# The second block's mixer: attention blocks, projections and delta steps written out side by side

## Chip, cores and metric

The kernel runs on one core of a Trainium2 chip. The metric is the device time of one execution in microseconds; the median of several runs counts. An engine is named as in the profile: PE (matmuls; PEld its weight loads), DVE (vector), ACT (activation functions), POOL (general vector work), SP (issues most DMAs).

## What is computed

Two transformer blocks of two layers each, over 512 tokens of width 1024, all in float32. The change touches only the mixer of the second block, which runs once in each of its two layers:

```python
u = rms_norm_2(x, pre_mix_w[l]) @ w_in[l]
(u_conv, dq, dk, dv, gqkv, gz, b_f, b_b, a_f, a_b) = jnp.split(u, offs, axis=-1)
y_conv  = conv_module(u_conv, ...)        # 31-tap depthwise convolution, layer norm, silu
y_diff  = diff_attention(dq, dk, dv, ...) # 6 heads: softmax(q1 k1 - slope*dist) - lam * softmax(q2 k2 - slope*dist), times v
y_delta = gated_deltanet(gqkv, gz, ...)   # 6 heads, both directions, chunks of 64: triangular solve, then a scan over 8 chunks
y = concatenate([y_conv, y_diff, y_delta]) @ w_out[l]
x = x + rms_norm_2(y, post_mix_w[l])      # then a feed-forward part of 4096 hidden columns
```

## The kernel before

The method `second(l)` is one layer of the second block. Activations lie feature by feature (128 partitions, 8 groups) as two tiles `hh` and `hl`, the high and low part of each float32; a matmul by a weight is three matmuls (`mm3`, L485 to L487; `bank`, L509, where the order of accumulation is fixed). A **dense unit** (`dense_fm`) is 128 output columns: its weights are loaded into `raw` (two buffers, pool `p_raw`), split into `wh` and `wl` (four buffers each, pool `p_whl`) by ACT, DVE and POOL, and multiplied in 24 matmuls of 512 columns. `dense_tok` makes 384 columns for all tokens in 96 matmuls.

The mixer's own parts, each for pairs of heads f = 0, 1, 2:

- `delta_proj` (three dense units: q, k, v), a 3-tap convolution and Silu, and transposes into `tokq`, `tokk`, `tokv`.
- `delta_prep`: norms, the decay matrices (tiles `E`), the products `KK`, a round through DRAM and the solve of 16x16 triangles (`delta_solve`, L1518 and L1520, 30 small DVE instructions), and the rest (`delta_prep2`: `Aq`, `kd`, `qg`).
- `delta_uw`: the inverse is put together from 16 to 32 to 64 rows, one direction d after the other and in the last stage one chunk c after the other; then U and W.
- `delta_scan`: both directions' chunk states step by step (copies L1650 on DVE, L1652 on ACT), then the output `OI`. `delta_out`: norm, gate, and a transpose into `cat` in DRAM.
- `conv_proj` (four units) and `conv_taps`: 31 taps, half on DVE (L1743), half by ACT (L1746) with POOL (L1747).
- `diff_proj` (six units, parked in DRAM as `qk`) and `diff`: 24 **blocks** (6 heads x 4 query blocks). `scores(b)` is two matmuls (L1840), a bias and minimum on DVE (L1842), Exp on ACT (L1844); `outputs(b)` combines the two halves (L1862 on DVE, or every third by ACT and POOL, L1859 and L1860), transposes (L1866), evacuates to `dat` and multiplies by `dv`.

Only dependences between tiles and the ring of buffers behind each tag are fixed. The order of each engine's instructions is set when the program is built, by a planner that at every moment prefers, of what it holds to be ready, what stands first in the program; so the written order is a priority. Before, `second` writes first all delta and dense work, then the attention. The attention's score tiles `dP` are taken from `p_raw`, its `dqk` and `dat` from `p_whl`, the buffers of the dense weights; its other tiles lie in the pool `rb`, which is opened when `hh` and `hl` are closed and takes their place. PSUM has four rings of two banks: `mm`, `fx`, `ax`, `sA`.

Of the kernel before, what the change touches and what calls it, by code (L numbers as in the profile page):

```python
# [17 lines left out]
P = 128  # L18
# [7 lines left out]
def shape_constants():  # L26
# [74 lines left out]
    c["dist"] = -np.abs(np.arange(896)[None, :] - 384 - i[:, None])  # L101
# [17 lines left out]
BAL = ((0, 0, 0), (0, 0, 0), (0, 0, 0))  # L119
# [56 lines left out]
class Kern:  # L176
# [1152 lines left out]
    def gates(self, l, pool, ps):  # L1329
# [10 lines left out]
        beta, a, e, u, g = T("beta"), T("ga"), T("ge_"), T("gu"), T("gg")  # L1340
# [41 lines left out]
    def delta_proj(self, l, f, pool, hsrc, pss=None):  # L1382

        nc = self.nc
        tok = [pool.tile([P, 4, 2, 64], F32, tag="tok" + n, name="tok" + n, bufs=1 if n == "q" else 2) for n in "qkv"]
# [17 lines left out]
        for z in range(3):  # L1403
# [4 lines left out]
        return tok  # L1408

    def delta_prep(self, l, f, pool, tok, G):  # L1410
# [15 lines left out]
        def normed(z, t):  # L1426
            x = pool.tile([P, 4, P], F32, tag="kq"[z] + "T", name="kq"[z] + "T", bufs=2 - z)
# [38 lines left out]
        KK = [pool.tile([P, 2, 4, 64], F32, tag=f"KK{d}", name="KK", bufs=2) for d in range(2)]  # L1466
# [25 lines left out]
    def delta_prep2(self, l, f, pool, st, E, normed, products, tq, tk, gb):  # L1492

        Aq = [pool.tile([P, 2, 4, 64], F32, tag=f"Aq{d}", name="Aq", bufs=2) for d in range(2)]
        products(normed(1, tq), [(Aq[d], E["q", d]) for d in range(2)])
        kd, qg = [], []
        for d in range(2):
            for lst, t, n, tag in ((kd, tk, "etl", "kd"), (qg, tq, "egc", "qg")):
                k = pool.tile([P, 4, 2, 64], F32, tag=f"{tag}{d}", name=tag, bufs=2)
                self.tt(k, t, gb(n, d), 512, ALU.mult)  # L1500
                lst.append(k)
# [26 lines left out]
    def delta_uw(self, l, f, pool, st, G):  # L1528
# [3 lines left out]
        st["U"], st["W"] = [], []  # L1532
        xd = st["xd"]
        Zs = [pool.tile([P, 8, 64], F32, tag=f"Z{d}", name="Z") for d in range(2)]
        TZ = [pool.tile([P, 2, 8, 32], F32, tag=f"TZ{d}", name="TZ") for d in range(2)]
        half = lambda i, n: self.half[:, i:i + 2].unsqueeze(1).unsqueeze(3).to_broadcast([P, n, 2, 512 // n // 2])
        for d in range(2):
# [5 lines left out]
        VBs = []  # L1543
        for d in range(2):
            v = pool.tile([P, 4, 2, 2, 64], F32, tag=f"VB{d}", name="VB")
            gb = lambda n: G[n][:, :, 6 * d + 2 * f:6 * d + 2 * f + 2].unsqueeze(3).to_broadcast([P, 4, 2, 64])
            self.tt(v[:, :, :, 0], st["tv"], gb("beta"), 512, ALU.mult)
            self.tt(v[:, :, :, 1], st["tk"], gb("beg"), 512, ALU.mult)
            VBs.append(v)
        for d in range(2):  # L1550
            Z, T, KK, VB = Zs[d], TZ[d][:, 0], st["KK"][d], VBs[d]
            hs = slice(6 * d + 2 * f, 6 * d + 2 * f + 2)

            GI = pool.tile([P, 8, 64], F32, tag=f"GI{d}", name="A16")
            self.mul(GI, KK.rearrange("p a b c -> p (a b) c"), self.dmc[:, 3 + d].unsqueeze(1).to_broadcast([P, 8, 64]), 512)
            blocks = [(slice(32 * q, 32 * q + 32), n) for n in range(8) for q in range(4)]
            pq = self.psx([P, 8, 32])
            for b, n in blocks:
                mm(pq[b, n], GI[b, n, b.start % 64:b.start % 64 + 32], T[b, n], start=True, stop=True)
            A = pool.tile([P, 2, 4, 32], F32, tag="Q", name="AT", bufs=2)  # L1560
            if d == 0:
                nc.vector.tensor_tensor(out=A, in0=pq.rearrange("p (h t) a -> p h t a", h=2),
                                        in1=G["beta"][:, :, hs].rearrange("p t h -> p h t").unsqueeze(3).to_broadcast([P, 2, 4, 32]), op=ALU.mult)
            else:
                nc.vector.tensor_copy(A, pq.rearrange("p (h t) a -> p h t a", h=2))
            A = A.rearrange("p h t a -> p (h t) a")
            pz = self.psx([P, 2, 8, 32])
            for b, n in blocks:
                mm(pz[b, 0, n], TZ[d][b, 1, n], A[b, n], start=True, stop=True)
                mm(pz[b, 1, n], A[b, n], TZ[d][b, 1, n], start=True, stop=True)  # L1570
            nc.vector.tensor_tensor(out=TZ[d], in0=TZ[d], in1=pz, op=ALU.subtract)
            self.load["dve"] += 900
            self.tt(Z.rearrange("p n (b j) -> p n b j", b=2), TZ[d][:, 1].unsqueeze(2).to_broadcast([P, 8, 2, 32]), half(0, 8), 512, ALU.mult)
            Q = pool.tile([P, 2, 4, 32], F32, tag="Q", name="Q", bufs=2)
            for c in range(2):
                s0 = 64 * c + 32 * d
                c0 = 64 * c + 32 * (1 - d)
                s_, c_ = slice(s0, s0 + 32), slice(c0, c0 + 32)
                sf, cf = slice(32 * d, 32 * d + 32), slice(32 * (1 - d), 32 * (1 - d) + 32)
                pq = self.psx([P, 2, 4, 32])  # L1580
                for h in range(2):
                    for tt in range(4):
                        mm(pq[c_, h, tt], KK[s_, h, tt, cf], T[s_, 4 * h + tt], start=True, stop=True)
                if d == 0:
                    nc.vector.tensor_tensor(out=Q[c_], in0=pq[c_], in1=G["beta"][c_, :, hs].rearrange("p t h -> p h t").unsqueeze(3)
# [209 lines left out]
    def diff(self, l, pool, qk, vd, cat, between):  # L1795
# [52 lines left out]
        def outputs(b):  # L1848
# [19 lines left out]
            if qb == 0:  # L1868
                s["po"], s["bank"] = self.psum([P, 4, 64]), self.bank()
# [492 lines left out]
```

## Time and profile before

| | |
|---|---|
| median of 3 runs | 4024.43 us (4018.16 to 4025.21) |
| the profiled execution | 4036.42 us; span from its first to its last instruction 4034.6 us |
| instructions | 67160 |
| DMA | 379.79 MB, mean 94 GB/s |

A row of the profile names a source line, an engine, an operation, and the tiles it writes and reads. "Busy" is the time in which the engine ran the instructions of a group, "idle before" the time in which it had nothing to run just before them, with what ended it. PEclk is the share of its full clock that TensorE was granted.

### The profile page before, as it was taken

Reading aid. Unit: us, or ns where it says so; the run is one execution under the profiler, and the core shown is the slowest. Engines: PE = TensorE matmul, PEld = TensorE weight load, DVE = VectorE, ACT = ScalarE, POOL = GpSimd, SP = SyncE. Lnnn points to the kernel's source line nnn. Section 1 sums busy time; section 2 is a strip of 40 time slices with the busy share of each in tenths; the row PEclk is TensorE's granted clock in tenths of the full one; section 3 lists DMA queues with packets and bytes.
Section 4 is the critical chain, followed back from the end, with each engine's and each line's share of the span. In section 5 each row is a group of like instructions: output and inputs, shape, how many; then the busy total and the mean of one; then the engine's idle time right before and its main releaser. Section 6 shows DMA issues by size and latency. Waiting matters only on the chain. (4 is left out here: it accounts for less than half of the span.)

```text
span 4034.6 us, 67160 instructions
## 1 busy us (share of the span) xinstructions
PE 3704.7 (92%) x27441; PEld 3287.6 (81%) x27441; DVE 2440.8 (60%) x4507; ACT 1571.0 (39%) x2654; POOL 1669.0 (41%) x1168
## 2 busy tenths in 40 slices
PE   8999989989998999997999988878999988878998
PEld 6888767989998788887999876768988776778988
DVE  6454566665666333336776684548767685558665
ACT  4544255323223222223343543444434443344433
POOL 2221225455553223233666454215554363115654
PEclk8999879989999999998999987879999887878999
DMA  6322444112222212121232433132334333132333
GB/s 208 93 77 78 155 130 157 43 53 65 72 73 77 66 58 71 60 84 51 84 115 88 118 99 119 52 113 94 105 105 122 92 101 104 55 123 92 105 97 112
DMA packets 420364, 379.79 MB, mean 94 GB/s; under 512 B 64586, under 2 KB 366169, under 8 KB 419161
## 3 DMA queue, kind: packets, MB, share of 16 engines
q1 hardware_dynamic: 414490, 367.01, 29.4%
q10 hardware_dynamic: 5567, 8.49, 0.6%
q8 instruction: 216, 3.54, 0.4%
q14 instruction: 91, 0.75, 0.1%
HBM read 332.21 MB, written 43.25 MB: 93 GB/s over the span
## 5 line engine op out<-in xcount | busy, mean ns | idle before, releaser
L206 ACT CAST wh<-raw 128x1024 fp32r<-128x1024 f32 (+2 forms) x441 | 444.6, 1014 | 630.9 <-PE mm L486 277.6
L233 POOL TENSOR_TENSOR wl<-raw,wh 128x1024 fp32r<-128x1024 f32 (+2 forms) x196 | 468.1, 2397 | 530.7 <-ACT wh L206 476.5
L233 DVE TENSOR_TENSOR wl<-raw,wh 128x1024 fp32r<-128x1024 f32 (+1 forms) x268 | 378.1, 1415 | 189.1 <-ACT wh L206 176.4
L485 PE MATMUL mm<-Hh,wh 128*128 128x512 f32 (+1 forms) x1256 | 417.5, 335 | 15.3 <-DVE x L1033 12.9
L487 PE MATMUL mm<-Hh,wl 128*128 128x512 f32 (+1 forms) x1256 | 417.0, 333 | 0.5 <-DVE wl L233 0.5
L486 PE MATMUL mm<-Hl,wh 128*128 128x512 f32 (+1 forms) x1256 | 416.3, 332 | 0.0
L485 PEld LDWEIGHTS mm<-Hh,wh 128*128 128x128 f32 x1256 | 238.7, 190 | 42.9 <-DVE x L1033 14.3
L487 PEld LDWEIGHTS mm<-Hh,wl 128*128 128x128 f32 x1256 | 238.8, 190 | 26.1 <-DVE wl L233 0.7
L486 PEld LDWEIGHTS mm<-Hl,wh 128*128 128x128 f32 x1256 | 239.0, 190 | 24.3
L485 PE MATMUL mm<-hh,wh 128*128 128x512 f32 (+1 forms) x640 | 231.9, 366 | 16.4 <-DVE hh L208 6.9
L509 PE MATMUL mm<-hl,wh 128*128 128x256 f32 (+1 forms) x808 | 231.5, 290 | 6.4 <-DVE hl L1960 6.3
L509 PE MATMUL mm<-hh,wl 128*128 128x256 f32 (+1 forms) x808 | 231.6, 290 | 5.5 <-DVE wl L233 4.1
L487 PE MATMUL mm<-hh,wl 128*128 128x512 f32 (+1 forms) x640 | 227.2, 357 | 2.8 <-POOL wl L233 2.8
L486 PE MATMUL mm<-hl,wh 128*128 128x512 f32 (+1 forms) x640 | 229.0, 359 | 0.6 <-DVE hl L698 0.6
L509 PE MATMUL mm<-hh,wh 128*128 128x256 f32 (+1 forms) x808 | 218.4, 288 | 6.5 <-ACT hh L1968 3.2
L206 ACT CAST wh<-s 128x1024 fp32r<-128x1024 f32 (+1 forms) x128 | 106.9, 835 | 267.4 <-PE mm L486 137.6
L509 PE MATMUL mm<-th,wh 128*128 128x256 f32 (+1 forms) x644 | 195.3, 305 | 8.1 <-ACT wh L206 5.5
L509 PE MATMUL mm<-th,wl 128*128 128x256 f32 (+1 forms) x644 | 197.3, 307 | 3.1 <-DVE wl L233 3.1
L1033 DVE SCALAR_TENSOR_TENSOR x<-mm,mod,x 128x512 f32<-128x512 f32 (+1 forms) x224 | 138.2, 630 | 99.9 <-PE mm L487 99.4
L509 PE MATMUL mm<-tl,wh 128*128 128x256 f32 (+1 forms) x644 | 195.3, 303 | 0.6 <-DVE tl L233 0.6
L233 POOL TENSOR_TENSOR Hl<-o,Hh 128x1024 fp32r<-128x1024 f32 (+3 forms) x76 | 140.9, 1856 | 92.6 <-ACT Hh L206 91.1
L509 PEld LDWEIGHTS mm<-hl,wh 128*128 128x128 f32 (+1 forms) x808 | 155.8, 193 | 9.7 <-DVE hl L1960 7.7
(737 smaller groups left out, 10886.8 us busy)
## 6 DMA issues: line engine op xcount, KB each, us to landing
raw<-in_w_ff_dram SPq DMA_DIRECT2D x68, 1024.0 KB
raw<-in_ffn_w_in_dram SPq DMA_DIRECT2D x88, 512.0 KB
raw<-in_mod_w_dram SPq DMA_DIRECT2D x40, 1024.0 KB
raw<-in_odd_w_in_dram SPq DMA_DIRECT2D x24, 1024.0 KB
raw<-in_ffn_w_out_dram SPq DMA_DIRECT2D x19, 1024.0 KB
raw<-in_w_in_dram SPq DMA_DIRECT2D x38, 512.0 KB
dqk<-qk SPq DMA_DIRECT2D x48, 256.0 KB
raw<-in_w_out_dram SPq DMA_DIRECT2D x12, 768.0 KB
```

The source lines that it names most:

```text
L206: nc.scalar.copy(hi, src)
L233: i = (nc.vector if e == "dve" else nc.gpsimd).tensor_tensor(out=out, in0=a, in1=b, op=op)
L485: mm(ps, ah, bh, start=first, stop=False)
L486: mm(ps, ah, bl, start=False, stop=False)
L487: mm(ps, al, bh, start=False, stop=last)
L509: i = self.nc.tensor.matmul(out, lhsT, rhs, start=start, stop=stop, skip_group_check=True)
L1033: self.nc.vector.scalar_tensor_tensor(out=x[:, ct, :n], in0=ps, scalar=gate[:, ct:ct + 1], in1=x[:, ct, :n], op0=ALU.mult, op1=ALU.add)
```

## The change

`second` now writes the attention's 24 blocks as the frame of the mixer. A head section makes the gates, f = 0 of the delta projections, the first q and k of the attention and all of `vd`. Then a table `steps` says which other work stands inside block b, between the scores of block b + 1 and the outputs of block b: one dense unit a block at most places, and one delta step.

- The attention has tiles of its own in the pool `dl`: `dqk` (three buffers), `dP` (two, one block each), `dat` (one). The slope is now the scale of the DVE instruction and divided out of q in `diff_proj` (`qs`), so that the biases on POOL go; all 24 combinations are on DVE. The products go into the transposes' bank (`fx`), and each block is scaled on its own (24 small DVE instructions for 6 larger).
- `KK`, `Aq`, `kd`, `qg` and `kqT` have one buffer where they had two.
- `delta_uw` handles both directions, and both chunks, together: one instruction for two or four.
- `conv_taps` stands after the last dense matmul, in `rb`, with four taps a block in blocks 13 to 20 and two buffers for `cm`. The pool `cv` goes.

```diff
-BAL = ((0, 0, 0), (0, 0, 0), (0, 0, 0))
+SLOPES = [2.0 ** -2, 2.0 ** -4, 2.0 ** -6, 2.0 ** -8, 2.0 ** -1, 2.0 ** -3]
...
-        KK = [pool.tile([P, 2, 4, 64], F32, tag=f"KK{d}", name="KK", bufs=2) for d in range(2)]
+        KK = [pool.tile([P, 2, 4, 64], F32, tag=f"KK{d}", name="KK") for d in range(2)]
...
+        A = pool.tile([P, 2, 8, 32], F32, tag="E", name="AT", bufs=5)
+        nc.vector.tensor_tensor(out=A.rearrange("p d n a -> p (d n) a"), in0=pq.rearrange("p d n a -> p (d n) a"),
+                                in1=bb.rearrange("p d h t -> p (d h t)").unsqueeze(2).to_broadcast([P, 16, 32]), op=ALU.mult)
...
+        for d, s_, c_, cf in places:
+            for h, tt in heads:
+                mm(pq[c_, h, tt], KK[d][s_, h, tt, cf], TZ[d][s_, 0, 4 * h + tt], start=True, stop=True)
+        Q = pool.tile([P, 2, 4, 32], F32, tag="Q", name="Q", bufs=2)
+        nc.vector.tensor_tensor(out=Q, in0=pq, in1=bm.unsqueeze(3).to_broadcast([P, 2, 4, 32]), op=ALU.mult)
...
+        def tap(t):
+            nc.vector.scalar_tensor_tensor(out=acc[:, 0], in0=hp[:, 0, t:t + 512], scalar=w(t, 0), in1=acc[:, 0], op0=ALU.mult, op1=ALU.add)
+            m = pool.tile([P, 512], F32, tag="cm", name="cm", bufs=2)
+            nc.scalar.activation(m, hp[:, 1, t:t + 512], AF.Copy, scale=w(t, 1))
+            nc.gpsimd.tensor_tensor(out=acc[:, 1], in0=acc[:, 1], in1=m, op=ALU.add)
...
-                t = self.p_whl.tile([P, 1024], F32R, tag="wh", name="dqk")
+                t = pool.tile([P, 1024], F32R, tag="dqk", name="dqk", bufs=3)
...
-            if b % 2 == 0:
-                blocks[b // 2] = (self.p_raw.tile([P, 2048], F32, tag="raw", name="dP").rearrange("p (q m c) -> p q m c", q=2, m=2),
-                                  self.p_whl.tile([P, 1024], F32R, tag="wl", name="dat").bitcast(F32).rearrange("p (q k c) -> p q k c", q=2, k=4))
-            pe = blocks[b // 2][0][:, b % 2]
+            pe = blocks[b] = pool.tile([P, 2, 512], F32, tag="dP", name="dP", bufs=2)
...
-            if b % 3 == 0:
-                nc.scalar.activation(pe[:, 1], pe[:, 1], AF.Copy, scale=rs[:, 1:2])
-                nc.gpsimd.tensor_tensor(out=pe[:, 0], in0=pe[:, 0], in1=pe[:, 1], op=ALU.add)
...
+            po = pt[:, 0, :64]
             for kb in range(4):
...
+            o = s["o"]
+            nc.vector.tensor_scalar(out=o[:, qb, h], in0=po, scalar1=rs[:, 0:1], scalar2=None, op0=ALU.mult)
...
             if b + 1 < nb:
                 scores(b + 1)
+            for f in steps.get(b, ()):
+                f()
             outputs(b)
...
+        for g in proj(0, pss[1:]):
+            g()
+        dp(0, 0)()
+        dp(0, 1)()
+        self.dense_tok(w, [(1280, 384)], [hs], park(vd), banks=[self.psum, self.psum, self.psf, self.psf])
         prep(0)
...
+        steps = {0: [p1[1]], 1: [p1[2]], 2: [p1[0], do(uw, 0)], 3: [dp(1, 0)], 4: [dp(1, 1), do(scan, 0), do(prep, 1)], 5: [p2[1]],
+                 6: [p2[2], do(uw, 1)], 7: [p2[0], cp(0)], 8: [dp(2, 0), do(scan, 1), do(prep, 2)], 9: [dp(2, 1)], 10: [cp(1), do(uw, 2)],
+                 11: [lambda: self.dense_tok(w, [(2816, 384)], [hs], park(zd, AF.Silu))], 12: [tail, do(out, 0), do(scan, 2)],
+                 13: [t4], 14: [t4, do(out, 1)], 15: [t4], 16: [t4, do(out, 2)], 17: [t4], 18: [t4], 19: [t4], 20: [t4]}
+        self.diff(l, pool, qk, vd, cat, steps, lambda f: None)
```

`proj(f)` gives the three units of `delta_proj`, `dp(f, z)` is `diff_proj` for q (z = 0) or k (z = 1), `cp(z)` is two units of `conv_proj`, `tail` closes `hh` and `hl`, opens `rb` and starts the convolution.

## Rows read from the trace of the kernel before

**Rows 1.** The page's first part: busy us, share of the span, instructions.
```profile
PE 3704.7 (92%) x27441; PEld 3287.6 (81%) x27441; DVE 2440.8 (60%) x4507; ACT 1571.0 (39%) x2654; POOL 1669.0 (41%) x1168
```
**Rows 2.** Windows: stretch, length, busy of five engines, PEclk, DMA share, GB/s.
```profile
2275.00:2455.00 180.00, 160.77 (x1313) 133.23 (x1312) 132.21 (x247) 86.64 (x130) 98.28 (x67) 0.91 0.40 112
2455.00:2641.00 186.00, 153.94 (x2800) 129.96 (x2798) 111.72 (x333) 73.51 (x175) 43.89 (x38) 0.78 0.22 65
2641.00:2687.50 46.50, 27.52 (x108) 22.87 (x108) 23.37 (x71) 18.02 (x33) 5.17 (x6) 0.50 0.45 153
2275.00:2687.50 412.50, 342.23 (x4219) 286.06 (x4217) 267.29 (x650) 178.17 (x337) 147.35 (x110) 0.81 0.33 95
...
3175.00:3585.40 410.40, 338.62 (x4218) 282.32 (x4217) 265.33 (x650) 177.73 (x336) 147.25 (x108) 0.81 0.33 96
...
2612.60:2633.90 21.30, 17.98 (x419) 17.07 (x418) 10.74 (x48) 7.12 (x18) 2.31 (x2) 0.90 0.14 48
...
2340.00:2400.00 60.00, 47.29 (x451) 43.26 (x450) 58.90 (x91) 28.95 (x43) 37.75 (x24) 0.83 0.33 77
```
**Rows 3.** Lines, first mixer, attention: count, busy us, mean ns, idle before, its ender.
```profile
L1844 ACT ACTIVATE dP<-dP,dmx 128x512 f32<-128x512 f32 x48 | 34.5, 720 | 66.5 <-DVE dmx L1842 64.3 <-DVE hy L645 2.2
...
L1842 DVE CUSTOM_DVE_ANT_0 dP<-fx,abias 128x512 f32<-128x512 f32 x48 | 32.5, 686 | 11.2 <-PE fx L1840 10.1 <-POOL abias L1809 0.6
...
L1862 DVE SCALAR_TENSOR_TENSOR dP<-dP,drs 128x512 f32<-128x512 f32 x16 | 14.2, 885 | 0.4
```
**Rows 4.** The same view: the convolution's taps.
```profile
L1747 POOL TENSOR_TENSOR cacc<-cacc,cm 128x512 f32<-128x512 f32 x30 | 43.4, 1448 | 37.0 <-ACT cm L1746 37.0
...
L1743 DVE SCALAR_TENSOR_TENSOR cacc<-hp,dw,cacc 128x512 f32<-128x512 f32 x30 | 32.8, 1094 | 0.7 <-ACT cacc L1739 0.6
```
**Rows 5.** Timeline, PE: dense matmuls in a row; then one block's transposes and products.
```profile
2441.15 0.40 PE L485 MATMUL mm<-hh,wh 128*128 128x512 f32 x1
2441.38 0.39 PE L486 MATMUL mm<-hl,wh 128*128 128x512 f32 x1
...
2603.85 0.66 PE L1866 MATMUL fx<-ident,dP 128*128 128x128 f32 x4
...
2605.91 1.10 PE L509 MATMUL mm<-dv,dat 128*128 128x64 f32 x8
```
**Rows 6.** Timeline, PE: the first mixer's end and the output projection's first matmuls.
```profile
2670.91 1.97 PE L509 MATMUL mm<-dv,dat 128*128 128x64 f32 x8 [0.68 <-ACT dat L243]
2682.95 1.12 PE L1707 MATMUL mm<-ident,do 128*128 128x128 f32 x4 [10.07 <-POOL do L233]
2687.53 2.50 PE L485 MATMUL mm<-hh,wh 128*128 128x512 f32 x5 [3.46 <-DVE hh L208]
```
**Rows 7.** Timeline, several engines: the delta chain of f=0, then of f=2.
```profile
2280.45 0.63 ACT L1417 ACTIVATE dsq<-tokq 128x512 f32<-128x512 f32 x1
...
2379.67 1.04 POOL L233 TENSOR_TENSOR TZ<-T,half 128x512 f32<-128x512 f32 x1 [0.51 <-DMA T<-xd]
...
2459.34 0.40 ACT L1606 ACTIVATE W<-ax 128x256 f32<-128x256 f32 x1
...
2459.50 0.65 PE L1431 MATMUL ax<-ident,tokk 128*128 128x128 f32 x4 [0.69 <-ACT U L243]
...
2495.70 0.62 ACT L1522 COPY chG<-chX 128x256 f32<-128x256 f32 x1 [2.94 <-DVE chX L1520]
...
2576.05 0.83 PE L1559 MATMUL ax<-TZ,A 32*32 32x32 f32 x64 [0.33 <-DVE o2n L644]
...
2612.14 0.40 ACT L1606 ACTIVATE W<-ax 128x256 f32<-128x256 f32 x1
...
2629.03 0.59 ACT L243 COPY OI<-ax 128x512 f32<-128x512 f32 x1 [2.84 <-PE ax L509]
```
**Rows 8.** Lines, ACT, first mixer: loads of function tables.
```profile
L1395 ACT ACT_TABLE_LOAD x2 | 2.6, 1283 | 0.0
...
L1844 ACT ACT_TABLE_LOAD x2 | 2.6, 1283 | 0.0
```

More of the change, by code (lines that the diff above doesn't have):

```diff
@@ L1402, in ev, with step @@
             return g
-        for z in range(3):
+        def step(z):
+            n = "tok" + "qkv"[z]
+            tok[z] = pool.tile([P, 4, 2, 64], F32, tag=n, name=n, bufs=2 if z else 1)
             if pss:
@@ new lines, in delta_uw @@
+        for d, s_, c_, cf in places:
+            o, i = Z[d][s_, :, cf], pz[s_].rearrange("p h t a -> p (h t) a")
+            if d:
+                nc.scalar.activation(o, i, AF.Copy, scale=-1.0)
+            else:
+                nc.vector.tensor_scalar(out=o, in0=i, scalar1=-1.0, scalar2=None, op0=ALU.mult)
+        self.load["dve"] += 3000
+        st["U"], st["W"] = ([pool.tile([P, 4, 2, 64], F32, tag=f"{n}{d}", name=n) for d in dd] for n in "UW")
+        VB = []
+        for d in dd:
@@ L1597, in delta_uw @@
+            VB.append(v)
+        for d in dd:
             for b in range(2):
@@ L1795, in diff, with ev @@
-    def diff(self, l, pool, qk, vd, cat, between):
+        def ev(j, i, ps):
+            hi, lo = (pool.tile([P, 512], F32, tag="pc", name=n, bufs=3) for n in ("dhi", "dlo"))
+            scale = 1.0 if z else self.qs[:, f:f + 1]
+            nc.scalar.activation(hi.bitcast(F32R), ps, AF.Copy, scale=scale)
+            nc.vector.scalar_tensor_tensor(out=lo.bitcast(F32R), in0=ps, scalar=scale, in1=hi, op0=ALU.mult, op1=ALU.subtract)
+            self.load["act"] += 480
+            self.load["dve"] += 662
+            for g in range(4):
+                nc.sync.dma_start(qk[f][z, g], lo if (g % 2, g // 2)[z] else hi)
@@ L2015, in out @@
         def out(f):
[L2016 to L2018 removed]
+            self.delta_out(l, f, late["rb"], OI[f], zd, cat[:, 5 + f], G)
         uw = lambda f: self.delta_uw(l, f, pool, sd[f], G)
[L2020 to L2028 removed]
@@ L2044, in second, with tail @@
-        out(1)
-        scan(2)
-        self.level(0, 0, 100)
-        out(2)
-        self.level(*BAL[2])
-        self.diff(l, rb, qk, vd, cat, lambda f: self.conv_norm(l, rb, acc, cat) if f == 1 else None)
-        p_rb.close()
-        p_cv.close()
+        dp = lambda f, z: lambda: self.diff_proj(l, f, z, pool, hs, qk)
+        cp = lambda z: lambda: self.conv_proj(l, z, pool, hs, hd)
+        do = lambda g, f: lambda: g(f)
+        def tail():
+            p_hs.close()
+            late["st"] = ExitStack()
+            late["rb"] = late["st"].enter_context(tc.tile_pool(name=f"rb{l}", bufs=1, side="right"))
+            late["acc"], late["taps"] = self.conv_taps(l, late["rb"], hd)
@@ new lines, in taps @@
+        def taps(n):
+            for _ in range(min(n, len(late["taps"]))):
+                late["taps"].pop(0)()
+            if not late["taps"] and late["acc"] is not None:
+                self.conv_norm(l, late["rb"], late["acc"], cat)
+                late["acc"] = None
+        for g in proj(0, pss[1:]):
[3 more added lines that the diff above has]
+        self.dense_tok(w, [(1280, 384)], [hs], park(vd), banks=[self.psum, self.psum, self.psf, self.psf])
+        prep(0)
+        p1, p2 = proj(1), proj(2)
```

245 lines of the change are left out of this document (88 added, 157 removed).

## The prediction

> **What bounds the kernel now.** I read the page's shares first [rows 1]. PE is busy for 92% of the span, which sounds like a kernel that only fewer matmuls could shorten. A share is a mean over stages, so next I cut the mixer out with the windows view [rows 2]. The first mixer is followed from 2275 us, when the shared first units are done, to 2687.5 us, when the output projection begins [rows 6]: 412.5 us; the second takes 410.4 us. Together they are a fifth of the span, and here nothing is full: PE 342 us of busy time at a granted clock of 0.81, DVE 267 us, ACT 178, POOL 147.
>
> The windows within it show two halves that lack what the other has. To 2455 us all dense units and much of the delta work run, PE is busy for 0.89 of the time at a clock of 0.91, and DVE for 0.73. From 2455 to 2641 us there is no dense unit left. Attention, scans and the late delta steps share the engines; PE's clock is 0.78, DVE's share 0.60. In the last 46.5 us the clock is 0.50 and both engines are half idle. The attention cannot begin sooner, whatever the planner wants: its tiles come out of `raw`, `wh` and `wl`, which the dense weights use until the last unit. The lines view says what such a stage waits for [rows 3]: ACT stands idle for 66.5 us before the 48 Exps, 64.3 of it until DVE has made the minimum. These are waits of a chain with nothing to put in between, not of a full engine.
>
> **What the mixer needs at least.** Busy time of PE at a low clock is stretched, so I multiply each stage's by its clock: 160.8 x 0.91 + 153.9 x 0.78 + 27.5 x 0.50 = 280 us at full clock (an estimate). At the busy share that PE reached in the first half, 0.89, that is 314 us. DVE's 267 us are less. So up to 98 us of each mixer is waiting that a better mixture could remove.
>
> **The change, part by part.**
>
> *Head section.* After 2275 us come two units of q and k and the 96 matmuls for `vd`. Dense matmuls follow each other every 0.23 us [rows 5]; for 384 columns I scale by 384/512. That is 48 x 0.233 + 96 x 0.175 = 28 us, on PE's path. The first dqk must go through DRAM, and the gates' small tiles now share the ring `E` with `prep(0)`; both delay only chains, under PE's 28 us and the next units. Without that cover each would cost what the chain is late, which no row shows; I set nothing.
>
> *Blocks 0 to 12, with the dense work.* What is left is 14 units and `zd`: 14 x 24 x 0.233 + 16.8 = 95 us, to which attention and delta add. The later blocks' PE work is 11 x 2.23 = 25 us (two scores at 0.233, four transposes 0.66, eight products 1.10 [rows 5]) and 16 us for one scan and the norms, from the window 2612.6 to 2633.9, where they ran nearly alone (18.0 busy at 0.90 [rows 2]). So this stage holds 280 - 28 - 41 = 211 us, at a share of 0.89 237 us.
>
> *Blocks 13 to 23.* No dense matmul is left, so DVE counts: 11 blocks at 2 x 0.686 + 0.885 and about 0.5 of small instructions [rows 3] are 31 us (24 instructions that scale the products, new, lie in that 0.5); 30 taps at 1.094 us [rows 4] are 33; scan, norms and conv_norm twice the 10.7 us of that window, 21. Together 85 us. At the first half's share, 0.73, they take 116 us, at the second half's, 0.60, 142. I take 116: the taps are independent work that can stand in the gaps, as they do in the first half.
>
> *The end.* Before, 16.6 us lie between the last block's products and the first output matmul [rows 6], as norm, transpose, `cat` and the split follow each other. That stays. But `hh` and `hl` no longer lie over the attention's tiles, and `raw` is free: the 48 matmuls on the convolution's rows, 11.2 us, and their weights can go in front. `x`, 2 MB, must now wait for the attention's pool; at the 153 GB/s of the last stretch [rows 2] that is 14 us beside 28 us of output matmuls, so nothing; uncovered it would be 14.
>
> *Edits inside the steps.* `delta_uw` becomes shorter as a chain: for f = 2 it took 36.5 us, 2576.05 to 2612.54, for two directions in turn [rows 7], and should take about half. POOL loses 8 combinations a mixer and the biases, DVE gains 8 x 0.885 = 7 us and loses about as much in `delta_uw`. POOL and ACT are far from full, so I count nothing. Of SP's queue: the same DMAs move; the weight loads now pass the reads of `dqk`, of which the third buffer lets only half of the next head be fetched ahead, so some of the five changes of head can hold SP and the loads behind it. No row prices that; between nothing and five loads late I take nothing, since `raw` has a second buffer.
>
> **The sum.** By parts: 28 + 237 + 116 + 16.6 - 11.2 = 386 us. This takes the stages one after the other. They are not: with tiles of its own the attention can run ahead of its place while PE is full, so DVE's later work moves forward. Were it all mixed, 314 + 16.6 - 11.2 = 319 us. With two `dP` buffers it can be only so far ahead; I take a point nearer the sum by parts, 361 us. Against 412.5 and 410.4 that gives 51.5 + 49.4 = 101 us. The profiled execution took 4036.4 us, so 3935; the median of the runs shown is 0.997 of it, so 3924 us.
>
> **The rivals.**
>
> *Everything mixes* (319 us a mixer): for it, the first half already reaches 0.89 on PE. Against it, this needs PE and DVE both above 0.83 throughout. 4036 - 185 = 3851, as a median 3840.
>
> *Table loads.* Exp, Silu and Sigmoid now alternate. Before, 48 Exps had two loads, of 1.28 us each [rows 8], because the dense evacuations were over. After, six evacuations of `delta_proj`, two of `conv_proj`, one group for `zd` and conv_norm each fall between Exps: 10 visits, 20 loads, 25.7 us a mixer. If all lie on the chain that paces the blocks, 361 becomes 387: 49 us saved, 3975 as a median. For it: ACT waits on the chain already [rows 3]; against it: ACT is busy for 178 of 412 us [rows 2], and a load can go ahead of the data.
> [...]
>
> *No gain.* The dense work runs ahead by itself, as the planner prefers whatever is ready, and the blocks from 13 on are paced as the second half was: 28 + 237 + 142 + 5.4 = 412 us, the time of before; 4024. For it: the planner has the same freedom before and after, and PSUM's `fx` ring of two banks serves scores, transposes, products and delta_proj alike. Against it: the later blocks hold one scan instead of three.
>
> *Slower: the delta chain.* With single `KK`, `kd`, `qg` and `Aq`, step f + 1 cannot pass step f: `prep` waits for `uw`, its rest for `scan`. One turn of f = 2 took 36 us from its first transposes to the solve's end, 36.5 us of `uw`, now half, and 16.5 us of `scan` [rows 7]: 71 us, some 80 with two trips through DRAM. With some 17 us for the last output that is 2280 + 3 x 80 + 17 = 2537, long before the attention's end. But f = 0, which met the taps on a DVE that was busy for 58.9 of 60 us [rows 2], took 179 us to the end of `uw` [rows 7]; with `uw` halved and a scan, 156. Three such turns end at 2765 us, 77 after 2687.5: 155 us slower, 4179 as a median. It decides from 130 us a turn. I expect about 100, as the taps have moved behind.
>
> **How the numbers follow.** Main case, 341 to 386 us a mixer, 0.46 (as medians 3884 to 3974); everything mixes 0.16; table loads 0.12; no gain, 395 to 425 us, 0.15; the chain 0.11. About 0.2% of the time, 8 us, is what a measurement of this kernel can tell from no change. Of "no gain" I give 0.06 to faster, 0.05 to same, 0.04 to slower. Faster: 0.46 + 0.16 + 0.12 + 0.06 = 0.80; same 0.05; slower 0.15. The range, 3845 to 4035, leaves out the chain, a third of "no gain" and the far end of the best case.
>
> **What the profile after would show.** Right: the attention's first scores within some 60 us of the head section's start, not behind the last dense unit; score instructions spread evenly over the mixer beside dense matmuls; PEclk above 0.85 in all but the last third; first output matmuls on `hh` before the last block's products. Wrong: PE waiting for delta tiles early in the mixer with ACT and DVE idle (the chain); 20 or more table loads with DVE waiting for Exp each time; dense matmuls over long before block 12, and a long stretch at DVE's 0.60 (no gain). What I may have wrong at the root is PE's need at full clock, since busy times of small matmuls overlap.

## The result, and the profile after

The changed kernel takes 4044.66 us (median of 4 runs, 4039.86 to 4047.34), the kernel before 4022.47 us in the same comparison: ratio 1.0055, 95% interval 1.0037 to 1.0072. It is slower, by 22 us; 3924 us and a range up to 4035 were forecast. Below, each kernel stands by its ratio to the kernel before on its own chip; differences in us are differences of ratios times 4022, and carry some 10 us of uncertainty.

The page's shares say nothing of it; PE even has 40 us less busy time than in [rows 1]:

```profile
PE 3664.5 (91%) x27441; PEld 3271.4 (81%) x27441; DVE 2416.8 (60%) x4523; ACT 1592.7 (39%) x2670; POOL 1670.1 (41%) x1164
```

The windows view does, cut as in [rows 2]: the part with the dense matmuls (the first score of block 13 follows at 2511), a hole, the last ten blocks, the end; then both mixers whole (421.5 us the second, up to its first output matmul as well). Columns: stretch, length, busy of PE, PEld, DVE, ACT, POOL, PEclk, DMA share, GB/s.

```profile
2275.00:2505.00 230.00, 207.78 (x2523) 178.09 (x2522) 130.62 (x352) 121.44 (x203) 86.03 (x64) 0.93 0.48 133
2505.00:2566.00 61.00, 27.10 (x414) 23.71 (x413) 53.64 (x66) 26.86 (x50) 46.97 (x31) 0.61 0.05 15
2566.00:2668.00 102.00, 81.75 (x1279) 69.78 (x1278) 67.87 (x225) 42.05 (x92) 14.53 (x11) 0.72 0.18 47
2668.00:2690.00 22.00, 2.99 (x13) 2.40 (x12) 3.61 (x17) 1.80 (x3) 2.30 (x2) 0.50 0.39 143
2275.00:2690.00 415.00, 319.62 (x4224) 273.98 (x4222) 255.74 (x659) 192.15 (x348) 149.84 (x107) 0.81 0.34 95
3175.00:3596.50 421.50, 323.40 (x4216) 275.99 (x4214) 254.43 (x653) 191.16 (x346) 149.84 (x107) 0.79 0.32 91
```

The two profiled executions are 11 us apart, not 22 (4047.3 and 4036.4; that of the kernel before lies above the median of its runs). Against [rows 2] the first mixer is 2.5 us longer and the second 11.1.

The first stage is as good as hoped: PE at a share of 0.90 and a clock of 0.93, with the scores of thirteen blocks of attention already in it. Then all is lost again. In the next 61 us PE works for 27, at a clock of 0.61, while DVE is busy for 53.6 and POOL for 47; in the 102 us behind them PE is busy for 82, at 0.72. The timeline of DVE shows the hole (start, us, engine, line, operation, tiles, count):

```profile
2514.33 0.68 DVE L1836 CUSTOM_DVE_ANT_0 dP<-fx,dist 128x512 f32<-128x512 f32 x1
...
2516.06 1.23 DVE L1705 TENSOR_SCALAR hss<-hss 128x8 f32<-128x8 f32 x1
2517.21 0.74 DVE L1752 SCALAR_TENSOR_TENSOR cacc<-hp,dw,cacc 128x512 f32<-128x512 f32 x1
2517.87 1.23 DVE L640 TENSOR_SCALAR hy<-hss 128x8 int32<-128x8 int32 x1
...
2519.74 1.22 DVE L1752 SCALAR_TENSOR_TENSOR cacc<-hp,dw,cacc 128x512 f32<-128x512 f32 x1
2520.89 1.23 DVE L642 TENSOR_SCALAR hy<-hy 128x8 int32<-128x8 int32 x1
...
2551.18 12.15 DVE L1752 SCALAR_TENSOR_TENSOR cacc<-hp,dw,cacc 128x512 f32<-128x512 f32 x8
...
2566.53 0.68 DVE L1836 CUSTOM_DVE_ANT_0 dP<-fx,dist 128x512 f32<-128x512 f32 x1
```

The 30 taps (L1752), written four to a block in blocks 13 to 20, all run ahead of block 14's score: the planner saw them ready and drew them forward. Between the second score of block 13 (2514.33) and the next score (2566.53) lie 52 us. And some small instructions are slow: a 128x8 operation takes 1.23 us. PE's timeline, in the same stretch, shows who waits:

```profile
2516.56 0.44 PE L1861 MATMUL fx<-dv,dat 128*128 128x64 f32 x2
...
2530.79 0.36 PE L510 MATMUL sA<-kd,GI 64*64 64x64 f32 x1 [6.25 <-DVE kd L1659]
...
2553.34 0.78 PE L1861 MATMUL fx<-dv,dat 128*128 128x64 f32 x6
```

Two of block 12's eight products ran at 2516.56, the other six at 2553.34. Between them stand, in the order that the planner gave PE's queue, the steps of scan(1), which wait for a copy (L1659) that stands behind taps in DVE's queue.

The delta chain can be read off the three outputs `OI` in ACT's timeline; before, the last of them was at 2629.03 [rows 7]:

```profile
2423.08 0.58 ACT L244 COPY OI<-ax 128x512 f32<-128x512 f32 x1 [2.85 <-PE ax L510]
...
2554.29 0.56 ACT L244 COPY OI<-ax 128x512 f32<-128x512 f32 x1
...
2656.32 0.59 ACT L244 COPY OI<-ax 128x512 f32<-128x512 f32 x1 [2.84 <-PE ax L510]
```

Counted from the square of `tokk` in the first norms (L1421, 2284.5) to the first `OI`, and then from one `OI` to the next, a turn of the chain takes 139, 131 and 102 us. The last one lies wholly behind the dense matmuls, and 13.6 us after it the last block's products end. The end, in PE's timeline and SP's queue, answers to [rows 6]:

```profile
2667.91 1.97 PE L1861 MATMUL fx<-dv,dat 128*128 128x64 f32 x8
...
2690.04 2.50 PE L486 MATMUL mm<-hh,wh 128*128 128x512 f32 x5 [12.07 <-DVE hh L209]
```

```profile
2680.79 0.32 SPq L2052 DMA_DIRECT2D x<-xs  x1
2681.16 0.90 SPq L2074 DMA_DIRECT2D ct<-cat  x2
```

From the end of the last products to the first output matmul 20.2 us pass instead of 14.6. SP issues the reload of `x`, 2 MB, just in front of the eight loads of `cat`, and no output matmul runs early.

### The profile page after: what moved, and what is told of

It reads as the page before. It is cut to its first block, busy times and chain, and to the rows that moved or that the text cites. A ratio compares the mean times of both kernels' runs of the same rounds, so it can differ in the third digit from the quotient of the medians.

```text
span 4045.5 us, 67262 instructions
## 1 busy us (share of the span) xinstructions
PE 3664.5 (91%) x27441; PEld 3271.4 (81%) x27441; DVE 2416.8 (60%) x4523; ACT 1592.7 (39%) x2670; POOL 1670.1 (41%) x1164
## 5 line engine op out<-in xcount | busy, mean ns | idle before, releaser
L234 POOL TENSOR_TENSOR wl<-raw,wh 128x1024 fp32r<-128x1024 f32 (+2 forms) x210 | 498.9, 2383 | 643.1 <-ACT wh L207 604.9
L234 DVE TENSOR_TENSOR wl<-raw,wh 128x1024 fp32r<-128x1024 f32 (+2 forms) x254 | 358.4, 1415 | 183.9 <-ACT wh L207 169.4
L486 PEld LDWEIGHTS mm<-hh,wh 128*128 128x128 f32 x640 | 124.9, 196 | 52.0 <-DVE hh L209 24.9
```

The source lines that it names most:

```text
L234: i = (nc.vector if e == "dve" else nc.gpsimd).tensor_tensor(out=out, in0=a, in1=b, op=op)
L486: mm(ps, ah, bh, start=first, stop=False)
```

## The experiments

All runs, by their ratio to the kernel before (95% interval), and their distance from the kernel after:

| kernel | ratio | interval | us from after |
|---|---|---|---|
| after | 1.0055 | 1.0037 to 1.0072 | 0 |
| 1. after, no taps | 0.9892 | 0.9870 to 0.9915 | -66 |
| 2. after, taps on DVE | 0.9982 | 0.9965 to 0.9998 | -29 |
| 3. after, taps spread | 0.9985 | 0.9970 to 1.0000 | -28 |
| 4. after, `cat` ahead of `x` | 1.0033 | 1.0018 to 1.0047 | -9 |
| 5. after, early taps | 1.0059 | 1.0041 to 1.0078 | +2 |
| 6. 5 and 4 | 1.0045 | 1.0032 to 1.0057 | -4 |
| 7. before, new `delta_uw` | 1.0021 | 1.0010 to 1.0032 | |
| 8. after, early prep | 1.0103 | 1.0086 to 1.0121 | +19 |
| 9. 8, 2, 3 and 4 | 0.9980 | 0.9970 to 0.9991 | -30 |
| 10. 8, no taps | 0.9905 | 0.9888 to 0.9923 | -60 |
| 11. after, filler | 1.0233 | 1.0217 to 1.0249 | +72 |
| 12. 13, early prep for f = 2 | 0.9981 | 0.9969 to 0.9993 | -30 |
| **13. 2, 3 and 4** | **0.9943** | 0.9926 to 0.9960 | **-45** |
| 14. 13, late `zd` | 0.9984 | 0.9974 to 0.9995 | -29 |
| 15. after, no third turn | 0.9851 | 0.9830 to 0.9872 | -82 |
| 16. before, no third turn | 0.9857 | 0.9842 to 0.9873 | |
| 17. before, no taps | 0.9931 | 0.9910 to 0.9952 | |
| 18. after, neither | 0.9652 | 0.9636 to 0.9669 | -162 |

The first theory was: the burst of taps, with no dense matmul to cover it, is the loss. Its rival: the serial delta chain sets the end.

**1. No taps.**
```diff
-        return acc, [lambda t=t: tap(t) for t in range(1, 31)]
+        return acc, []
```


> The kernel after, with the 30 taps of the late convolution left out (its first tap, the norm and the write to cat stay, so the convolution's part of the output is not the reference's). Theory (the taps run in one burst once the dense matmuls are over, and hold scan(1) and through PE's queue the attention): the 55 us hole between the scores of blocks 13 and 14 shrinks to some 10 to 15 us, 40 to 50 us a mixer, so 3945 to 3965 us. Rival (the delta chain with single buffers paces the tail, the taps only fill its waits): the hole stays for the greater part, at most 15 us a mixer, so 4015 to 4045 us.

66 us (3973.98 us, median): between the two, and the hole between the scores of blocks 13 and 14 shrank from 55 to 27 us, not to 10. ACT's timeline of `OI`, and PE's last products:

```profile
2417.17 0.58 ACT L244 COPY OI<-ax 128x512 f32<-128x512 f32 x1 [2.85 <-PE ax L510]
...
2522.41 0.58 ACT L244 COPY OI<-ax 128x512 f32<-128x512 f32 x1 [2.58 <-PE ax L510]
...
2620.39 0.59 ACT L244 COPY OI<-ax 128x512 f32<-128x512 f32 x1 [2.84 <-PE ax L510]
...
2632.98 1.97 PE L1861 MATMUL fx<-dv,dat 128*128 128x64 f32 x8
```

The turns are 136, 105 and 98 us, the second 26 us shorter and the others hardly, and the last products still follow the chain's end, by 14.6 us. Both theories hold in part.

**2. All taps on DVE.**
```diff
-            m = pool.tile([P, 512], F32, tag="cm", name="cm", bufs=2)
-            nc.scalar.activation(m, hp[:, 1, t:t + 512], AF.Copy, scale=w(t, 1))
-            nc.gpsimd.tensor_tensor(out=acc[:, 1], in0=acc[:, 1], in1=m, op=ALU.add)
+            nc.vector.scalar_tensor_tensor(out=acc[:, 1], in0=hp[:, 1, t:t + 512], scalar=w(t, 1), in1=acc[:, 1], ...)
```


> The kernel after, with both halves of the taps on DVE: 60 instructions there, none of them on ACT and POOL. If it is DVE's own load that makes the burst, DVE's work in it grows by 30 x 0.75 = 22 us and the kernel gets slower by 10 to 22 us a mixer: 4065 to 4090 us. If it is DVE and POOL holding each other up (128x8 instructions of DVE take 1.23 us beside POOL's taps, 0.17 us elsewhere), the burst gets no longer or shorter, since 60 x 0.75 = 45 us stand against the 52 us that the DVE half alone takes now: 4015 to 4050 us, and the 128x8 instructions are back at 0.17 us.

Better than either: DVE does twice the taps and the kernel is 29 us faster. (This run, and 9, 12, 13 and 14, also double the taps in the planner's account of DVE's load, by which it gives shared work to one engine or another.) Lines of DVE from 2500 to 2570 us (count, busy us, mean ns, idle before), first after, then this run, where 27 of the first half's 30 taps fall into that window:

```profile
L1752 DVE SCALAR_TENSOR_TENSOR cacc<-hp,dw,cacc 128x512 f32<-128x512 f32 x30 | 35.4, 1179 | 5.3 <-ACT cacc L1746 4.8
...
L1705 DVE TENSOR_SCALAR hss<-hss 128x8 f32<-128x8 f32 x1 | 1.2, 1233 | 0.0
```

```profile
L1752 DVE SCALAR_TENSOR_TENSOR cacc<-hp,dw,cacc 128x512 f32<-128x512 f32 x27 | 21.6, 798 | 4.9 <-ACT cacc L1746 4.8
...
L1705 DVE TENSOR_SCALAR hss<-hss 128x8 f32<-128x8 f32 x1 | 0.2, 165 | 0.0
```

One tap falls from 1179 to 798 ns and the 128x8 instructions that took 1230 to 160. So POOL's taps held DVE's, and much of what stood among them.

**3. Taps spread over their blocks.**
```diff
+            self.order(<tap on DVE>, self.last)     # the last score instruction written before it
+            self.order(<ACT's product>, self.lastx) # the last Exp written before it
```


> The kernel after, with each group of four taps held by an order behind the scores of its own block, on DVE and ACT, so that the planner can't draw all thirty into one burst; no work is added or left out. Theory (the burst's place is the fault): the hole of 55 us goes, the taps cost what DVE has no gap for, and 15 to 35 us a mixer come back: 3975 to 4015 us. Rival (the tail has as much work for DVE and POOL as it can hold, wherever it stands; or the delta chain paces it): the time stays, 4035 to 4055 us.

28 us, 14 a mixer, at the lower edge of the theory's range: the place of the burst counts, but less than half of what leaving out the taps gives comes back.

**4. `cat` ahead of `x`.**
```diff
-            nc.sync.dma_start(x, xs)
...
                 self.split(hh[:, k], hl[:, k], t, 512)
+            nc.sync.dma_start(x, xs)
```


> The kernel after, with the reload of x (2 MB) issued behind the eight loads of cat instead of in front of them. Theory (in SP's queue the reload delays the closing, where the first split waits 15.28 us for its cat tile): 4 to 8 us a mixer, so 4028 to 4037 us. Rival (the closing waits for the last attention output's own way through DRAM, and the reload only lies beside it): no change, within 4 us of after.

9 us, as expected. In SP's queue and PE's timeline the end is 14.9 us long again:

```profile
2678.97 0.80 SPq L2073 DMA_DIRECT2D ct<-cat  x2
2679.82 0.42 SPq L2075 DMA_DIRECT2D x<-xs  x1
...
2666.07 1.97 PE L1861 MATMUL fx<-dv,dat 128*128 128x64 f32 x8
...
2682.93 1.65 PE L486 MATMUL mm<-hh,wh 128*128 128x512 f32 x3 [6.79 <-DVE hh L209]
```

**5 and 6. Early taps, alone and with 4.**
```diff
-        VB = []
+            v = pool.tile([P, 4, 2, 2, 64], F32, tag="VB", name="VB")    # one for both directions
...
+        def tap(t):
+            lo, hi = max(0, 15 - t), min(512, 527 - t)
+            i = nc.vector.scalar_tensor_tensor(out=acc[:, lo:hi], in0=hp[:, lo + t - 15:hi + t - 15], ...)
+            self.order(i, self.last)
...
+        steps = {..., 3: [dp(1, 0), cp(0)], 4: [..., tz(0, 6)], 5: [p2[1], tz(0, 8)], ..., 7: [p2[0], cp(1), tz(0, 8)],
+                 8: [..., tz(1, 6)], 9: [dp(2, 1), tz(1, 8)], 10: [do(uw, 2), tz(1, 8)], 11: [..., tz(1, 8)], 12: [tail, ...], 13: [norm], ...}
```


> The kernel after, with its convolution early again: each half of the channels is projected (blocks 3 and 7) and filtered by itself, on DVE alone, in two tiles of the attention's pool (blocks 4 to 11, each group behind the scores of its block); the room comes from one VB tile for both directions of delta_uw. Only conv_norm stays in the tail. Theory (the taps were the wrong work to leave for a stretch without dense matmuls): DVE is idle for 100 of the first 230 us, the 45 us of taps find room there, and the tail runs as it did without taps (3974 us): 3960 to 3995 us. Rival (DVE's gaps in the first part are waits of the delta chain, which the taps lengthen, and that chain ends the mixer): the tail begins 20 us or more later, 4010 to 4050 us.

> The same with the reload of x behind the loads of cat. The two edits lie in stages that follow each other, so the 11 us of the reload add to what the early taps give: 3949 to 3984 us, 8 to 14 us below the early taps alone. If the tail now ends in another wait (the last scan in front of the last products), the closing is the same and they add all the same; if cat is late for another reason, nothing.

The rival was right. ACT's `OI`:

```profile
2421.10 0.59 ACT L244 COPY OI<-ax 128x512 f32<-128x512 f32 x1 [2.29 <-PE ax L510]
...
2544.66 0.59 ACT L244 COPY OI<-ax 128x512 f32<-128x512 f32 x1 [2.85 <-PE ax L510]
...
2645.10 0.59 ACT L244 COPY OI<-ax 128x512 f32<-128x512 f32 x1 [2.84 <-PE ax L510]
```

The second output comes 276 us after the first norms, 241 without taps: beside dense matmuls, attention and the delta chain the taps cost the first part 35 us, as much as in the tail. (The shared `VB` is in this too.) But the 60 taps were not the 45 us of work that was counted on; DVE's lines show equal taps at very different prices:

```profile
L1745 DVE SCALAR_TENSOR_TENSOR cacc<-hp,dw,cacc 128x500 f32<-128x500 f32 x4 | 5.3, 1330 | 0.0
...
L1745 DVE SCALAR_TENSOR_TENSOR cacc<-hp,dw,cacc 128x501 f32<-128x501 f32 x4 | 2.9, 730 | 0.0
```

All 60 took 57.7 us: 21 ran beside an instruction of POOL, which splits weights in this part, and took 1.38 us in the mean, the other 39 took 0.74. So run 2's hold is here again, from other work of POOL; what early taps would cost without it was not tried. The reload behind `cat` (run 6) gives 6 us more, below its 9 alone and the 8 to 14 expected, but within the uncertainty.

**7. The new `delta_uw` in the kernel before.** Its diff is that function.

> The kernel before, with the change's delta_uw alone (both directions side by side). For f = 2 it took 36.5 us before and 27 us in the kernel after. If the delta chain holds the attention in the second half, 5 to 9 us a mixer: 4004 to 4013 us. If the attention's own blocks set the end there, nothing: 4018 to 4028 us.

No gain, rather 8 us lost. In its trace the last `OI` starts at 2573, 56 us earlier than before, and the last products at 2671.15 as against 2670.91 [rows 6]: the delta chain is not what the second half of the kernel before waits for. Where the 8 us come from stays open.

**8 and 10. First part of `delta_prep` in front of the scan, with and without taps.**
```diff
-        3: [dp(1, 0)], 4: [dp(1, 1), do(scan, 0), do(prep, 1)], ..., 7: [p2[0], cp(0)], 8: [dp(2, 0), do(scan, 1), do(prep, 2)]
+        3: [do(prep, 1), dp(1, 0)], 4: [dp(1, 1), do(scan, 0), do(rest, 1)], ..., 7: [p2[0], do(prep, 2), cp(0)], 8: [dp(2, 0), do(scan, 1), do(rest, 2)]
```


> The kernel after, with the first part of delta_prep (up to the triangular solve) written in front of the scan before it, and only its second part (Aq, kd, qg, whose single buffers the scan still reads) behind it. No tile is added. Theory (the chain of delta steps, one turn after the other, ends the mixer: with taps or without, the last output OI of f = 2 comes 98 to 102 us after that of f = 1, and the last products 13 to 18 us after it): the 36 to 40 us from one OI to the end of the next solve lie beside the scan and delta_uw of the step before, and 20 to 40 us a mixer come back: 3965 to 4005 us. Rival (only the work that DVE has in the tail counts, taps among it): nothing, 4035 to 4055 us.

> The first kernel of this call (first part of delta_prep early) with the 30 taps left out as in the run without taps, so that the convolution's part of the output is not the reference's. Without taps the chain stood alone at the end (3974 us). Theory: with the chain 20 to 40 us shorter, 3900 to 3940 us. Rival (without taps it is the attention's own pace or PE that ends the mixer): 3960 to 3980 us.

8 is slower than either theory had it (with taps, the solve of f = 2 falls into the burst and takes from 2539 to 2584), 10 no faster than without the edit. The theory that the chain alone ends the mixer fell. `OI` and the last products without taps:

```profile
2445.58 0.59 ACT L244 COPY OI<-ax 128x512 f32<-128x512 f32 x1 [0.78 <-PE ax L510]
...
2547.95 0.59 ACT L244 COPY OI<-ax 128x512 f32<-128x512 f32 x1 [6.17 <-PE ax L510]
...
2606.35 0.59 ACT L244 COPY OI<-ax 128x512 f32<-128x512 f32 x1 [2.84 <-PE ax L510]
...
2641.51 1.97 PE L1861 MATMUL fx<-dv,dat 128*128 128x64 f32 x8 [0.73 <-ACT dat L244]
```

The last turn is 58 us instead of 98, and the last products come at 2641.5, later than before the edit (2633.0; the first unit began 3.5 us sooner here). What the chain gained, others paid: the first output moved from 136 to 168 us, and behind the last `OI` 37 us of blocks were left instead of 15. I read this as the same work standing in the queues in another order; no run tests that reading by itself.

**9, 12 and 13. The edits together.** 9 is 2, 3, 4 and 8; 13 leaves out 8; 12 has 8 for f = 2 alone.

> The same, with all taps on DVE and spread over their blocks, and the reload of x behind the loads of cat: the three edits that gave 31, 31 and 11 us alone. If the chain and the taps hold the end one after the other, they add in part: 3920 to 3970 us. If the shorter chain only lets the taps' load set the end, 3970 to 4000 us.

> The kernel after with all taps on DVE, spread over their blocks, the reload of x behind the loads of cat, and the first part of delta_prep in front of the scan for f = 2 alone. Writing it early for f = 1 had moved the end of scan(0) from 136 to 168 us, beside dense matmuls; for f = 2 alone that loss should go while the turn of f = 2 stays at 58 to 77 us. Expected: the last products 15 to 25 us earlier than with both early (379 us), 3968 to 3995 us. If the work of the tail, not the chain, sets its end, as much as the next run.

> The same without the early first part of delta_prep: the kernel after with all taps on DVE, spread, and the reload of x behind the loads of cat. Theory (the taps' burst, the hold of POOL's taps on DVE, and the closing): without taps the mixer took 28 us less than before, DVE's spread taps cost 14 of them at the end, and the closing gives 5 a mixer: 3985 to 4000 us. If spreading and moving to DVE mend the same 31 us, 4000 to 4010 us.

13 is the best kernel: 3996.08 us, 45 us below after and 23 below before. 2 and 3 mend mostly the same loss (29 + 28 + 9 = 66 alone). With the early `delta_prep` 9 and 12 are both 15 us worse, outside what was expected of them, as 10 was. The windows of 13's first mixer, cut after the same 230 us:

```profile
2260.40:2490.40 230.00, 208.83 (x2532) 178.77 (x2531) 133.65 (x355) 121.74 (x203) 87.02 (x64) 0.93 0.48 134
2490.40:2657.60 167.20, 106.32 (x1700) 92.14 (x1700) 116.10 (x326) 50.54 (x115) 26.09 (x22) 0.65 0.15 41
2260.40:2657.60 397.20, 315.15 (x4232) 270.91 (x4231) 249.75 (x681) 172.27 (x318) 113.11 (x86) 0.81 0.34 95
```

The first part is that of after to a few us; the rest takes 167 us instead of 185.

**11. Filler matmuls, against the low clock.**
```diff
+                if f and n:
+                    self.order(mm(self.psum()[:, :256], self.ident, self.dist[:, :256], start=True, stop=True), i)
...
+                for _ in range(2) if b > 12 else ():
+                    self.order(nc.tensor.matmul(self.psum()[:, :256], self.ident, self.dist[:, :256], start=True, stop=True), i)
```


> The kernel after with 68 more matmuls a mixer whose results nobody reads (ident against 256 columns of dist, in the free bank ring of the dense units): one behind every step of scan(1) and scan(2), two behind every score matmul from block 13 on. Theory of the clock (PE stands at about half clock in the hole, 27 us of work there and 82 us behind it are stretched at 0.61 and 0.72, and that is what makes the tail long): if the filler lifts the clock there to 0.9 or more, PE's 109 us shrink by some 25 to 30 and 5 to 25 us a mixer come back, the filler's own time paid: 3995 to 4035 us. Rival (PE's clock is low because it waits; the tail is set by what DVE and the queues hold): the filler costs up to its own time, 4045 to 4080 us.

72 us slower, outside both ranges, and not a clean answer: the planner moved the last dense matmuls from 2495 to 2560 and the burst of taps behind them, and blocks 16 and 17 stand 99 us apart. Windows of the hole and of seven late blocks, and five late blocks of run 10 without filler:

```profile
2590.00:2640.00 50.00, 21.26 (x320) 18.73 (x320) 48.19 (x70) 18.42 (x34) 35.78 (x22) 0.60 0.04 11
2663.10:2695.00 31.90, 30.24 (x193) 26.86 (x191) 24.00 (x84) 16.80 (x40) 2.31 (x2) 0.97 0.12 42
```

```profile
2613.30:2636.00 22.70, 19.84 (x70) 15.13 (x71) 14.23 (x40) 10.16 (x24) 2.21 (x2) 0.50 0.10 35
```

In the late blocks the clock is 0.97 with filler and PE busy for 0.95 of the time; without, it is 0.50, and PE is at 0.87 (in the traces of before and after the clock's records hold 1.00 and 0.50 alone). A block takes 4.6 us and 4.5 us. So there the clock was nearly twice as high with filler and a block no shorter; that the filler raised it is a reading of these two kernels. In the hole the clock stayed at 0.60. How long the tail would be at full clock without such work stays open.

**14. `zd` late.**
```diff
-                 11: [<zd>], 12: [tail, do(out, 0), do(scan, 2)], 13: [t4], 14: [t4, do(out, 1)], ...
+                 12: [do(scan, 2)], 13: [<zd>], 14: [tail, do(out, 0)], 15: [t4, do(out, 1)], 16: [t4], 17: [t4, do(out, 2)], ...
```


> The kernel with all taps on DVE, spread, and the reload of x behind the loads of cat (3996 us), with the unit for zd, 96 dense matmuls, moved from block 11 to block 13, and what needs the place of hh and hl (the tail's pool, taps, outputs) two blocks later. Theory (the first part is full of PE work, share 0.9, and the tail has gaps on PE): the 17 us of zd leave the first part and cost 2 to 10 in the tail: 3966 to 3988 us. Rival (the tail's start is moved by as much, since taps and outputs wait for hh and hl to be free): 3996 to 4020 us.

The last products come 4 to 7 us earlier than in 13, but the first output matmul 3 to 6 us later, as taps, norm and outputs stand at the very end: 16 us worse by the ratios, of which the two mixers of the traces show 8.

**15, 16, 17 and 18. What the third turn and the taps cost in each kernel.**
```diff
-8: [dp(2, 0), do(scan, 1), do(prep, 2)], ... 10: [cp(1), do(uw, 2)]
+8: [dp(2, 0), do(scan, 1)], ... 10: [cp(1)]       # and scan(2) returns at once
```
16 leaves the same three steps out of the kernel before; 17 runs its loop over the taps for none; 18 is 15 and 1 together.

> The kernel after, without delta_prep, delta_uw and delta_scan of f = 2 (its projections stay; a copy of the output of f = 1 takes its place, so that part of the output is not the reference's). It tells what the third turn of the delta chain costs where it stands, behind the dense matmuls. Theory (the third turn lies wholly in the tail and the last blocks stand behind it in PE's queue): 45 to 60 us a mixer, 3925 to 3955 us. Rival (it lies beside the taps and the attention, which set the end by themselves): at most 15 us a mixer, 4015 to 4045 us.

> The same work of f = 2 left out of the kernel before (with the same consequence for the output). If the third turn costs there what it costs in the kernel after, the change has not brought it under cover: 3900 to 3932 us. If before hides the most of it (parts of it ran beside dense matmuls there), 3950 to 4000 us, and the difference is what the change lost by leaving the turn to the tail.

> The kernel before, with its 60 tap instructions (30 for each half of the channels) left out, so that the convolution's part of the output is not the reference's. In the kernel after the taps cost 35 us a mixer. Theory (the change took them from a place where they were nearly covered to one where they are not): 0 to 15 us a mixer here, 3990 to 4022 us. Rival (they cost as much in either place, as DVE's work is on the path there too): 3940 to 3965 us.

> The kernel after, without the taps and without delta_prep, delta_uw and delta_scan of f = 2 (both parts of the output are then not the reference's). Alone they cost 35 and 45 us a mixer. If they lie one after the other on what ends the mixer, the prices add: 3875 to 3895 us. If they lie in part beside each other, the sum is larger than their costs alone (either hides the other): 3840 to 3870 us. If the attention's own blocks set the end then, the sum is smaller: 3900 to 3950 us.

The third turn costs 82 us after and 57 before; the taps 66 and 28. After, the two add (162 together, 148 by themselves, within the uncertainty), so each lies on what ends the mixer. The third turn's price is a little under what its theory had (41 us a mixer). Before hid 25 of the 82 us: run 16 lies in the range for "hides the most of it", but the words don't fit. The taps were nearly covered before, as their theory had it. Without both, from block 13's first score to the start of the last products 71 us pass:

```profile
2518.40:2589.80 71.40, 54.76 (x223) 43.13 (x221) 45.77 (x166) 33.36 (x71) 0.00 (x0) 0.55 0.14 48
2489.50:2589.80 100.30, 79.30 (x729) 66.28 (x728) 59.55 (x209) 47.64 (x104) 0.18 (x2) 0.63 0.21 69
```

The second line begins at the last dense matmul, 29 us earlier; scan(1) runs in those 29 us.

## Why the prediction was wrong

Against the sum, for the first mixer:

| term | forecast | measured |
|---|---|---|
| head section and blocks 0 to 12 | 28 + 237 = 265 | 236 |
| blocks 13 to 23 | 116 | 157 |
| end | 16.6 | 22 |
| output matmuls in front | -11.2 | 0 |
| mixing (386 to 361) | -25 | 0 |
| sum | 361 | 415 |

**The step that failed is the place of the third delta step.** *Blocks 13 to 23* gave the tail one scan, taps, norms and eleven blocks, 116 us, and left the rest of the delta work, `delta_prep` and `delta_uw` of f = 2 with it, to *Blocks 0 to 12*. But it doesn't run there. The prediction expected turns of about 100 us; the first two take 139 and 131. PE's timeline of after shows the last dense matmul, the start of scan(1), and the third turn's first transposes:

```profile
2495.08 0.34 PE L488 MATMUL mm<-wh,hl 128*128 128x384 f32 x1
...
2511.22 2.03 PE L1646 MATMUL ax<-kd,W 64*64 64x64 f32 x32 [5.40 <-ACT U L244]
...
2552.51 0.99 PE L1435 MATMUL ax<-ident,tokk 128*128 128x128 f32 x4
```

So two scans lie behind the dense matmuls instead of one, and the third turn has its products `L1`, its solve, `delta_uw` and scan only after 2554, over 50 us behind the last of them. Left out, that turn gives back 41 us a mixer with the taps in place (run 15) and 48 without them (18 against 1). The stage took 157 us. By run 18 the taps and the third turn are 81 of them, and without both 71 are left; the other 5 lie within the uncertainty.

Those 71 us equal the forecast of the rest, (85 - 33) / 0.73 = 71, but in part by luck. In run 18 scan(1) was over before block 13's first score, so that no scan lies in them, and DVE was busy for 45.8 us at a share of 0.64, not for 52 at 0.73. Counted from the last dense matmul the rest took 100 us.

The first stage is 29 us shorter than forecast. PE's busy time multiplied by the clock, as the prediction reckons, is 207.8 x 0.93 = 193 us to 2505, where the forecast put 28 + 211 = 239, and 27.1 x 0.61 + 81.8 x 0.72 = 75 behind it, where it put 25 + 16 = 41 (an estimate, from the windows of after; in before the same eight products took 1.10 us at a clock of 1.00 and 1.97 at 0.50 [rows 5, 6]). So work stood behind the stage that was counted in it; no run tests that this is the whole of the 29 us.

**Taps "as independent work that can stand in the gaps"** had the price about right and the reason wrong. The term gave them 33 / 0.73 = 45 us; they cost 33 (run 1) to 40 (18 against 15) a mixer. They didn't fill gaps: they ran in one burst, DVE's and POOL's holding each other (1.18 us a tap and 1.55 us an addition in the mean; in before 0.74 for 22 taps with nothing of POOL beside them and 1.29 for 12 additions with DVE mostly idle), and stopped scan and attention. Before, they cost 14 us a mixer. And the 1.094 us a tap [rows 4] was itself a price beside POOL's additions; where nothing of POOL ran beside it a tap took 0.74 (those 22; the second half's 30 in run 13 took 0.74 in the mean).

**Mixing** gave nothing in the sum. The choice of 361 over 386 supposed that blocks run ahead of their place. They came as written: block 13 after the last dense matmuls.

**The end.** The 48 matmuls in front never ran: the output's PSUM banks and `x` lie where the attention's tiles do, `hh` and `hl` where `rb` does. This is read from the code and the trace, not tried. The reload of `x`, set at nothing, costs 4.4 us a mixer.

**What held.** The dense part ran at PE's share of 0.90 (0.89 forecast), the first scores came 34 us after the section's start, PEclk was 0.93 there. Table loads did double, from 14 to 27 in the first mixer, but only two of them lie after 2500 us: so that rival is out for the tail. Each of the 27 took 1.28 us of ACT; no run here prices them in the first part.

**The rivals.** The serial chain, with a chance of 0.11, came nearest in the profile: its turns are 124 us in the mean, where about 100 were expected, just under the 130 from which it was to decide. But its mechanism isn't the whole of it: shorter last turns (runs 8, 10 and 12) brought no earlier end. What costs is the turn's work behind the dense part, in the same queues as the last blocks; that it is the queues is read from the traces. Why the first two turns take over 130 us beside the dense matmuls was not tested, but the taps are 26 us of the second (run 1).

**Why slower than before.** Taps 38 us dearer, the third turn 25, the end 9: 72 us. The change lost 22, so its other parts gave some 50 back (a difference, not a run, and each term carries some 10 us): presumably the attention of blocks 0 to 12 under the dense matmuls.

## What to carry to other kernels

Before putting work in a stage of a sum, follow its chain: a step belongs where its inputs are ready, not where it is written, and a serial chain's turn times its turns says what is left when the cover ends. Work that was hidden has a price of its own in the new place; leave it out of both kernels and compare. And give a planner's ready work an order, or it will come in one piece.

## What the runs showed of the hardware

In the burst of after, seven 128x8 instructions of DVE took 1.22 to 1.23 us, each beside POOL's additions (mean 1.55 us for 512 columns); five others took 0.15 to 0.16 us in the two pauses of POOL (2530.4 to 2533.2 and 2536.1 to 2538.3), and one at 2519.01, as one addition ended. 30 DVE taps took 35.4 us with POOL's taps (after) and 23.8 without (run 2). The score instructions, which read one operand from PSUM, took 0.68 us beside an addition (2514.33) as with POOL idle (2566.53). No run shows by what the two engines hold each other.

Other work of POOL than DVE's own partner slowed taps too: in before, one beside a weight split took 1.99 us (2377.71) and one beside `kd` 1.55 (2338.49). Early taps beside the weight splitting took 57.7 us for 60, late ones 45.7 (runs 5 and 13). DVE was idle for 100 of the first 230 us of after, and still the taps cost the mixer 35 us there, in a run that also shared `VB`.
